# A four-layer encoder trunk on one core: other places for the modulation sums, the biases, the pooling product, and the second attention's key projection first

## The chip, the cores and the metric

The kernel runs on one core of one Trainium2 chip. The metric is device time in microseconds of one execution. Each time is the median of several runs; beside them one execution was taken by the hardware profiler, and all rows below come from that one. The engines: PE (TensorE, matmuls; PEld are its weight loads), DVE (VectorE), ACT (ScalarE), POOL (GpSimd), SP (SyncE, which issues most transfers).

## The reference

The input is x of 256 tokens by 1024 channels, one conditioning vector c, and the weights of four layers. Layer i mixes tokens by i mod 3: 0 is latent attention (layers 0 and 3), 1 a convolution module (layer 1), 2 a pooling mixer (layer 2); each is followed by a squared-ReLU feed-forward of width 4096.

```
c_act = silu(c)
for i in range(4):
    sh_m, sc_m, gt_m, sh_f, sc_f, gt_f = split(c_act @ ada_w[i] + ada_b[i], 6)
    h = rmsnorm(x, g0) * (1 + sc_m) + sh_m
    y = attention(h) | conv(h) | pool(h)
    x = x + gt_m * rmsnorm(y, g1)
    h = rmsnorm(x, g2) * (1 + sc_f) + sh_f
    x = x + gt_f * rmsnorm(relu(h @ w1) ** 2 @ w2, g3)
```

The attention projects h down to 384 columns for the queries and 256 + 32 for keys and values, norms both, projects them up for 16 heads, and applies a rotary embedding to 32 columns of each head. The convolution module is a gated product of 1024 to 2048 columns, 31 causal taps per channel, a layer norm, silu and a product of 1024 by 1024 with bias. The pooling mixer takes windowed means less the token, and multiplies four groups of 256 channels by their own matrix, with bias and scale.

## The kernel before, in words

The tokens are two tiles of 128. Every float32 product is made of three passes in the fp32r form: a weight is split into a high part (`A.copy`, L173) and a low part (`V.tensor_tensor`, L174), so is each activation, and a product is high by high, low by high and high by low (`mm3`, L582). So every weight tile of 512 KB that arrives costs ScalarE and DVE about a microsecond each. Weights go through five buffers (`NRAW`), their halves through six each (`NHL`).

**Boundaries.** `boundary` (L522) stands between any two sub-layers: squares of y, root on POOL, residual, squares of x, root, scaled tokens, transposes. The two tiles go one after the other. `line` fixes the order on an engine. For the convolution and the feed-forwards a `headblock` runs the first weight block for tile 0 ahead of tile 1's transposes; for the second attention and the pooling mixer nothing stands there. The pooling mixer hands in `tokens` and `early` in place of transposes.

**Modulation.** `c_act @ ada_w` is cut into 88 units of 1 MB that run beside the layers (8 more at the start): unit n is piece n mod 8 of a row group; the groups are, by layer, (g0, g1, g2) and then (g0, g2, g1). `ada(n)` takes n units at the places that the lists `MIX` and `FF` give: for a mixer the units at its places, those in the boundary ahead of it, and those fetched ahead; for a feed-forward the units after each of 16 chunks, and the same two. A unit is either 4 matmuls on PE, or two accumulates on DVE (L221, L223), after which one flush (`ada_flush`) multiplies the sums on PE. In feed-forwards and in the convolution the units go to DVE, in boundaries and in the pooling mixer to PE. After the last piece the row goes through DVE and, when it is needed, over DRAM into a broadcast tile (`spread`, two transfers on POOL's queue).

**Buffers of the units.** There are four (`NADA`). A unit's transfer is issued by SP, and SP issues in the order in which the program is written; it waits for a free buffer, and what stands behind it waits too. In a feed-forward `ada_fetch(ahead)` stands at chunk 14 (`CF`), behind the chunk's own unit and ahead of the fetch of the second-product weights of chunk 13. `tc.issue_after(gli.ins)` puts a chunk's units on DVE behind its `gl` (L710).

**Feed-forward** (L682): 16 chunks of 256 hidden columns; chunk c's first product (`colhalf`, L646), relu, square, halves; then the second product of chunk c - 1 (`rowblock`, L660) into four banks `y`; the last one takes chunks 14 and 15.

**Second attention** (L786): `down` runs the keys' and the queries' down projections in turn, two pieces of 128 rows at a time; then both are normed (`stats`, `normed`, `gained`).

**Convolution** (L1040): eight blocks of the gated product with the taps of an earlier block between them, then the last taps, layer norm (`un`), transposes, silu, and the product with `w_pw2` in two halves; its bias is 8 matmuls with one row, high and low.

**Pooling mixer** (L1177): means by a band matrix on PE, halves, then for each tile its bias (4 one-row float32 matmuls in the trace) and 24 matmuls of 256 columns.

## Time and profile before

| what | us |
|---|---|
| median of 3 runs | 1178.71 (1175.62 to 1179.85) |
| the profiled execution | 1184.47 |
| its span, first to last instruction | 1182.6 |
| PE busy | 1138.4 |
| PEld busy | 923.5 |
| DVE busy | 850.6 |
| ACT busy | 645.3 |

Engines run beside each other; PE's busy time counts an instruction until its modelled end, and overlapping ones once. The mean granted TensorE clock of this execution is 0.983 of full speed (2.4 GHz). The stages, by the span: first attention to 157 us, feed-forward 0 to 340, convolution to 470, feed-forward 1 to 662, pooling mixer to 690, feed-forward 2 to 883, second attention to 988, feed-forward 3 to the end.

### The profile page before, as it was taken

Reading aid. Unit: us, or ns where it says so; the run is one execution under the profiler, and the core shown is the slowest. Engines: PE = TensorE matmul, PEld = TensorE weight load, DVE = VectorE, ACT = ScalarE, POOL = GpSimd, SP = SyncE. Lnnn points to the kernel's source line nnn. Section 1 sums busy time; section 2 is a strip of 40 time slices with the busy share of each in tenths; the row PEclk is TensorE's granted clock in tenths of the full one; section 3 lists DMA queues with packets and bytes.
Section 4 is the critical chain, followed back from the end, with each engine's and each line's share of the span. In section 5 each row is a group of like instructions: output and inputs, shape, how many; then the busy total and the mean of one; then the engine's idle time right before and its main releaser. Section 6 shows DMA issues by size and latency. Waiting matters only on the chain. (4 is left out here: it accounts for less than half of the span.)

```text
span 1182.6 us, 17593 instructions
## 1 busy us (share of the span) xinstructions
PE 1138.4 (96%) x6706; PEld 923.5 (78%) x6706; DVE 850.6 (72%) x1197; ACT 645.3 (55%) x1145; POOL 54.1 (5%) x127
## 2 busy tenths in 40 slices
PE   7899999999999999999999999999997999999997
PEld 4667778788778867888887677878877878888886
DVE  3689787877766665787876778787876995755554
ACT  3355576556553244755564366555545675756553
POOL 1000010000010010000000110000011001000000
PEclk9999999999999988999999899999998999999999
DMA  9878759787617785778896479888644522766550
GB/s 332 304 290 311 298 208 347 270 329 290 245 53 236 256 322 213 272 272 351 315 343 256 187 278 364 311 311 323 246 134 157 170 81 80 250 199 191 183 193 35
DMA packets 73383, 290.00 MB, mean 245 GB/s; under 512 B 9986, under 2 KB 15234, under 8 KB 61012
## 3 DMA queue, kind: packets, MB, share of 16 engines
q1 hardware_dynamic: 70484, 280.44, 65.1%
q0 software_dynamic: 2816, 8.46, 2.0%
q8 instruction: 52, 0.85, 0.3%
q14 instruction: 31, 0.25, 0.1%
HBM read 286.57 MB, written 2.29 MB: 244 GB/s over the span
## 5 line engine op out<-in xcount | busy, mean ns | idle before, releaser
L174 DVE TENSOR_TENSOR lo<-raw,hi 128x1024 fp32r<-128x1024 f32 (+2 forms) x335 | 392.0, 1192 | 98.4 <-ACT hi L173 69.0
L173 ACT CAST hi<-raw 128x1024 fp32r<-128x1024 f32 (+2 forms) x335 | 335.1, 1028 | 78.6 <-PE y L587 39.4
L652 PE MATMUL h<-hT,hi 128*128 128x512 f32 x960 | 240.4, 392 | 0.0
L652 PEld LDWEIGHTS h<-hT,hi 128*128 128x128 f32 x960 | 175.8, 188 | 37.7 <-issue 3.4
L583 PE MATMUL y<-hi,gh 128*128 128x512 f32 x512 | 200.3, 393 | 1.5 <-ACT hi L173 1.5
L586 PE MATMUL y<-lo,gh 128*128 128x512 f32 x512 | 200.1, 391 | 0.2
L587 PE MATMUL y<-hi,gl 128*128 128x512 f32 x512 | 199.0, 390 | 0.0
L655 PEld LDWEIGHTS h<-hT,lo 128*128 128x128 f32 x960 | 131.0, 190 | 14.9 <-issue 5.9
L704 ACT COPY r<-h 128x256 f32<-128x256 f32 x120 | 44.5, 371 | 175.8 <-PE h L655 175.7
L655 PE MATMUL h<-hT,lo 128*128 128x256 f32 x960 | 136.0, 283 | 0.0
L223 DVE SCALAR_TENSOR_TENSOR acc<-araw,c_act,acc 128x1024 f32<-128x1024 f32 x106 | 130.7, 1279 | 0.4 <-DMA araw<-in_ada_w_dram 0.4
L583 PEld LDWEIGHTS y<-hi,gh 128*128 128x128 f32 x512 | 96.3, 188 | 22.8 <-ACT hi L173 2.4
L587 PEld LDWEIGHTS y<-hi,gl 128*128 128x128 f32 x512 | 96.1, 188 | 21.8 <-issue 0.8
L586 PEld LDWEIGHTS y<-lo,gh 128*128 128x128 f32 x512 | 96.4, 188 | 18.5 <-DVE lo L174 1.0
L705 DVE TENSOR_TENSOR r<-h,r 128x256 f32<-128x256 f32 x120 | 50.5, 421 | 39.8 <-ACT r L704 39.2
L710 DVE TENSOR_TENSOR gl<-r,gh 128x512 fp32r<-128x512 f32 x60 | 41.4, 690 | 50.2 <-ACT gh L709 50.2
L706 ACT ACTIVATE r<-r 128x512 f32<-128x512 f32 x60 | 37.9, 632 | 35.2 <-DVE r L705 35.2
L583 PE MATMUL y<-hi,hT 128*128 128x512 f32 x96 | 39.4, 412 | 0.0
L707 ACT ACTIVATE r<-r 128x512 f32<-128x512 f32 x60 | 37.9, 632 | 1.7
L586 PE MATMUL y<-lo,hT 128*128 128x512 f32 x96 | 38.8, 405 | 0.0
L587 PE MATMUL y<-hi,hT 128*128 128x512 f32 x96 | 38.6, 404 | 0.0
L709 ACT CAST gh<-r 128x512 fp32r<-128x512 f32 x60 | 37.2, 620 | 1.4
(257 smaller groups left out, 1486.8 us busy)
## 6 DMA issues: line engine op xcount, KB each, us to landing
raw<-in_w_dram SPq DMA_DIRECT2D x256, 512.0 KB, 5.8
araw<-in_ada_w_dram SPq DMA_DIRECT2D x96, 1024.0 KB, 6.4
raw<-in_w_pw_dram SPq DMA_DIRECT2D x24, 512.0 KB, 5.7
raw<-in_w_o_dram SPq DMA_DIRECT2D x16, 512.0 KB, 3.2
u<-ud SPq DMA_DIRECT2D x32, 132.0 KB, 2.8
raw<-in_w_ukv_dram SPq DMA_DIRECT2D x8, 512.0 KB
bc_g<-rowd POOLq DMA_DIRECT2D x8, 512.0 KB, 4.0
bc_a<-rowd POOLq DMA_DIRECT2D x7, 512.0 KB, 6.7
```

Of the source, the lines that this page charges most:

```text
L173: put(A.copy(h, raw), "act")
L174: put(V.tensor_tensor(l, raw, h.bitcast(F32), op=ALU.subtract), "dve")
L223: V.scalar_tensor_tensor(acc, raw[:, sl], ck, acc, op0=ALU.mult, op1=ALU.add)
L583: mm = T.matmul(o, ah, bh, start=start, stop=False, skip_group_check=True)
L586: T.matmul(o, ah, bl, start=False, stop=False, skip_group_check=True)
L587: return T.matmul(o, al, bh, start=False, stop=stop, skip_group_check=True)
L652: T.matmul(b, w(0, kk), pair[:, :, kk], start=(kk == 0), stop=False, skip_group_check=True)
L655: T.matmul(b[:, 0:S], w(1, kk), pair[:, 0, kk], start=False, stop=(kk == KT - 1), skip_group_check=True)
L704: A.copy(rf, hb[:, S:])
L705: V.tensor_tensor(rf, hb[:, 0:S], rf, op=ALU.add)
L706: A.activation(r, r, AF.Relu)
L710: gli = V.tensor_tensor(gl, g2, gh.bitcast(F32), op=ALU.subtract)
```

## The change

- A finished modulation row is written to DRAM at once (`stage`); a broadcast is then one transfer.
- The four matmuls of a unit or flush stand in the order 2, 3, 0, 1 and are chained.
- The pooling boundary: the second tile's y-squares come ahead of the first tile's means; the casts of the means, the first tile's bias and the high part of its product come between the second tile's steps; the mixer's order on PE is written out.
- Biases of convolution and pooling: `bias_rows` puts high and low on rows 0 and 32 of one tile; 2 matmuls per token tile with a `ones_r` of 33 rows, in the convolution in the middle of the product.
- The convolution fetches the first four pieces of `w_pw2` in its loop, and broadcasts and turns the next rows at m == 2; its ninth place for units is gone.
- The pooling constants are fetched ahead of feed-forward 1 and not in its chunk 12; the first weights of feed-forward 2 ahead of the units.
- The lists of units: fewer in boundaries and mixers, more in the feed-forwards 0 and 1, and there up to chunk 14.
- The second attention: `downblock` loads two of the four key pieces ahead of the boundary, runs them for tile 0 ahead of tile 1's transposes, then the other three quarters, then norms the keys; the queries' projection follows. One of the two key banks comes from the "h" banks.

```
@@ -244,6 +244,10 @@
...
+        for j in ((0, 1) if g == 1 else (1,)):
+            stage(i, g, j)
+        if (i, g) == (2, 0):
+            stage(i, g, 0)
@@ -261,9 +265,13 @@
...
-        for j in range(4):
+        mm = None
+        for j in (2, 3, 0, 1):
+            prev = mm
...
+            if prev is not None:
+                nosync(mm, prev)
@@ -538,15 +552,16 @@
...
-            if tokens is not None:
-                tokens(xa, r)
-                low = early()
-            else:
+            if tokens is None:
...
+        if tokens is not None:
+            tokens(xa, r)
...
+        if tokens is not None:
+            low = early()
@@ -561,13 +576,17 @@
...
+        if tokens is not None:
+            low[0][0]()
...
+            low[1][0]()
+            early()
...
-            low[0]()
+            low[0][1]()
...
-            low[1]()
+            low[1][1]()
@@ -657,6 +676,19 @@
...
+    def bias_rows(src, gain=None):
+        raw = raws.tile([P, D], F32, tag="raw", name="bias")[0:33]
+        G.memset(raw, 0.0)
+        for p in (0, 32):
+            nc.sync.dma_start(raw[p:p + 1], src)
+        if gain is not None:
+            V.tensor_tensor(raw, raw, gain[0:33], op=ALU.mult)
+        r = raws.tile([P, D], F32R, tag="raw", name="bias_r")[0:33]
+        A.copy(r, raw)
+        V.tensor_tensor(r[32:33], raw[32:33], r[32:33].bitcast(F32), op=ALU.subtract)
+        return r
@@ -783,7 +815,32 @@
...
-    def mla(i, h, units, ahead):
+    def downblock(w, hh, hl):
+        src, width = w.rearrange("p k n -> p (k n)"), KVL + ROPE
+        parts = [load(src[:, width * kk:width * (kk + 2)]) for kk in (0, 2)]
+        bs = []
+        def run(t, ks):
+            if len(bs) == t:
+                bs.append(bank("y" if t else "h", f"ck{t}"))
+            ts = slice(t * P, (t + 1) * P)
+            for low in range(2):
+                for kk in ks:
+                    if kk // 2 == len(parts):
+                        parts.append(load(src[:, width * kk:width * (kk + 2)]))
+                    wh, wl = parts[kk // 2]
+                    c = slice((kk % 2) * width, (kk % 2 + 1) * width)
+                    for st, mv in ((hl, wh),) if low else ((hh, wh), (hh, wl)):
+                        line("pe", T.matmul(bs[t][:, :width], st[:, kk, ts], mv[:, c],
+                                            start=(not low and kk == 0 and mv is wh),
+                                            stop=(low == 1 and kk == KT - 1),
+                                            skip_group_check=True))
+            return bs
+        return run
+    def mla(i, h, units, ahead, first=None):
@@ -850,11 +907,21 @@
...
-            dkv = down(w_dkv[j].rearrange("p k n -> p (k n)"), KVL + ROPE, "ck")
...
-            for _ in range(4):
-                ckb = next(dkv)
-                cqb = next(dq)
+            if first is None:
+                dkv = down(w_dkv[j].rearrange("p k n -> p (k n)"), KVL + ROPE, "ck")
+                for _ in range(4):
+                    ckb = next(dkv)
+                    cqb = next(dq)
+            else:
+                first(1, (0, 1, 2, 3))
+                first(0, (4, 5, 6, 7))
+                ckb = first(1, (4, 5, 6, 7))
+                last.clear()
+                rk = stats(ckb, KVL)
+                ckh, ckl = gained(normed(ckb, KVL, rk, "ck"), kg, "ck")
+                for _ in range(4):
+                    cqb = next(dq)
@@ -1087,6 +1157,12 @@
...
+                else:
+                    for k in range(2):
+                        fetch(w_pw2[j, 2 * (m + 2 - KT) + k])
+                if m == 2:
+                    prep(i, 2)
+                    shift_rows()
@@ -1109,39 +1185,32 @@
-            b2h, b2l = load(b_pw2[j])
             wp = [load(w_pw2[j, k]) for k in range(4)]
+            bias = bias_rows(b_pw2[j])
+            ada_flush()
...
-            prep(rows[(i, 2)])
-            shift_rows()
...
-            ada(units[8])
-            ada_flush()
...
-                for n in range(2):
-                    ns = slice(512 * n, 512 * n + 512)
-                    T.matmul(y[t][n], ones_r, b2h[:, ns], start=True, stop=False, skip_group_check=True)
-                    T.matmul(y[t][n], ones_r, b2l[:, ns], start=False, stop=False, skip_group_check=True)
@@ -1158,7 +1227,11 @@
...
-                     [sl_[:, k] for k in range(4)], y, False, False, tiles_first=True)
+                     [sl_[:, k] for k in range(4)], y, True, False, tiles_first=True)
+            for t in range(NT):
+                for n in range(2):
+                    T.matmul(y[t][n], ones_r, bias[:, 512 * n:512 * n + 512], start=False,
+                             stop=False, skip_group_check=True)
@@ -1206,73 +1276,94 @@
...
+        def product(t, low):
+            ts = slice(t * P, (t + 1) * P)
+            for g in range(4):
+                for k in range(2):
+                    ws = slice((2 * (g % 2) + k) * 256, (2 * (g % 2) + k) * 256 + 256)
+                    for q in ((0, 1), (0,))[low]:
+                        line("pe", T.matmul(y[t][g // 2][:, 256 * (g % 2):256 * (g % 2) + 256],
+                                            (ph, pl)[low][:, 2 * g + k, ts], wp[g // 2][q][:, ws],
+                                            start=False, stop=(low == 1 and k == 1),
+                                            skip_group_check=True))
+        def biased(t):
+            for n in range(2):
+                line("pe", T.matmul(y[t][n], ones_r, bias[:, 512 * n:512 * n + 512],
+                                    start=True, stop=False, skip_group_check=True))
+        y = []
+        spilt = []
-            low = [means(0, h) for h in range(2)]
-            ahead1.append(means(1, 0))
-            return low
+            if not spilt:
+                parts = [means(0, h) for h in range(2)]
+                spilt.append(spill(0))
+                return parts
+            y.extend(y_banks())
+            biased(0)
+            product(0, 0)
...
         head(tokens=tokens, early=early)
+        for k in range(2):
+            fetch(w1[i, 0, k])
+        ada_fetch(ahead)
+        spilt.append(spill(1))
+        parts = [means(1, h, spilt[h]) for h in range(2)]
+        for high, _ in parts:
+            high()
+        for _, low in parts:
             low()
         gate["free"] = 0
+        gate_row(i)
+        prep(i, 2)
+        biased(1)
+        product(0, 1)
+        product(1, 0)
+        product(1, 1)
         ada(units)
...
     MIX = {
         0: ([2, 4, 2, 3, 3, 2], 0, 1),
-        1: ([0, 0, 2, 0, 1, 2, 1, 0, 1], 2, 3),
-        2: (2, 4, 3),
+        1: ([0, 0, 2, 1, 1, 1, 1, 0, 0], 1, 3),
+        2: (1, 4, 2),
         3: ([0, 0, 0, 0, 0, 0], 0, 0),
     }
     FF = {
-        0: ([1, 1, 1, 1, 1, 2, 1, 1, 1, 1, 1, 1, 1, 1, 0, 0], 1, 3),
-        1: ([1, 1, 1, 2, 1, 1, 2, 1, 1, 2, 1, 1, 1, 1, 0, 0], 2, 4),
-        2: ([1, 1, 1, 1, 2, 1, 2, 1, 2, 1, 1, 2, 1, 2, 1, 0], 2, 0),
+        0: ([1, 2, 1, 1, 2, 1, 1, 2, 1, 1, 2, 1, 1, 2, 1, 0], 1, 3),
+        1: ([2, 1, 1, 2, 1, 1, 2, 1, 1, 1, 1, 1, 1, 1, 1, 0], 2, 4),
+        2: ([1, 1, 1, 1, 1, 1, 1, 1, 1, 1, 2, 1, 1, 2, 2, 0], 1, 0),
         3: ([0] * NFC, 0, 0),
     }
     qgs = cp.tile([P, q_g.shape[0], 3], F32, name="qgs")
@@ -1299,6 +1390,9 @@
...
+            elif s:
+                run = downblock(w_dkv[i // 3], hi, lo)
+                first = [lambda t: run(t, (0, 1, 2, 3)), run]
```

Left out are the calls that pass (i, g, j) in place of a row, `ones_r` with 33 rows, `spill` and `means` (the two halves of the former `means`), and the transfer of the pooling constants.

## Rows read from the trace of the kernel before

**Rows 1.** The page's first part: busy time, share, instructions.

```profile
PE 1138.4 (96%) x6706; PEld 923.5 (78%) x6706; DVE 850.6 (72%) x1197; ACT 645.3 (55%) x1145; POOL 54.1 (5%) x127
```

**Rows 2.** Stretches: busy PE, PEld, DVE, ACT, POOL; granted clock, DMA share, GB/s.

```profile
436.70:450.40 13.70, 13.70 (x42) 8.69 (x35) 7.54 (x14) 7.06 (x18) 1.17 (x2) 0.50 0.86 348
450.40:468.60 18.20, 18.20 (x82) 15.00 (x80) 10.69 (x12) 7.47 (x14) 1.56 (x3) 1.00 0.62 232
...
672.20:682.50 10.30, 10.30 (x36) 7.53 (x35) 4.96 (x9) 0.96 (x3) 3.22 (x6) 0.50 0.67 277
...
890.70:894.10 3.40, 3.40 (x15) 2.83 (x15) 2.14 (x7) 2.59 (x9) 1.52 (x3) 0.50 0.17 46
```

**Rows 3.** Timeline of PE, feed-forwards 0 and 1: start us, us, what, [idle before].

```profile
221.02 1.05 PE L265 MATMUL adap<-acc,ones_c 128*32 128x512 f32 x4
...
222.67 1.05 PE L265 MATMUL adap<-acc,ones_c 128*32 128x512 f32 x4
...
309.32 0.39 PE L652 MATMUL h<-hT,hi 128*128 128x512 f32 x1
...
631.37 1.98 PE L652 MATMUL h<-hT,hi 128*128 128x512 f32 x8
...
637.01 1.07 PE L265 MATMUL adap<-acc,ones_c 128*32 128x512 f32 x8
639.60 1.19 PE L583 MATMUL y<-hi,gh 128*128 128x512 f32 x4 [1.52 <-ACT hi L173]
```

**Rows 4.** Timeline of PE, the convolution's product and the units behind it.

```profile
439.44 0.78 PE L583 MATMUL y<-hi,hT 128*128 128x512 f32 x1
...
468.87 1.92 PE L265 MATMUL adap<-araw,c_act 128*32 128x512 f32 x16
```

**Rows 5.** Timeline of ACT in the pooling mixer.

```profile
668.64 0.60 ACT L135 ACTIVATE junk<-y 128x512 bf16<-128x512 f32 x1
...
685.31 0.60 ACT L135 ACTIVATE junk<-y 128x512 bf16<-128x512 f32 x1
```

**Rows 6.** Timeline of PE in the pooling mixer.

```profile
673.32 3.78 PE L1251 MATMUL y<-raw,ones_f 1*128 1x512 f32 x4
```

**Rows 7.** Timeline of DVE at the convolution's tail.

```profile
433.16 2.35 DVE L174 TENSOR_TENSOR lo<-raw,hi 128x1024 fp32r<-128x1024 f32 x2
...
436.42 0.81 DVE L1132 TENSOR_SCALAR un<-ctok,mv,r 128x512 f32<-128x512 f32 x1
```

**Rows 8.** Waits of PE, 877 to 920 us: total us, times, longest.

```profile
PE hT_ps L412 <- DVE xa L406: 3.6, 1, 3.6
PE cqT L836 <- DVE cn L832: 2.5, 1, 2.5
```

**Rows 9.** Timeline of DVE behind the second attention's boundary.

```profile
894.99 3.82 DVE L174 TENSOR_TENSOR lo<-raw,hi 128x576 fp32r<-128x576 f32 x5
```

**Rows 10.** Timeline of DVE, accumulates of chunk 13 in feed-forwards 0 and 1.

```profile
309.07 2.47 DVE L223 SCALAR_TENSOR_TENSOR acc<-araw,c_act,acc 128x1024 f32<-128x1024 f32 x2
...
629.55 2.48 DVE L223 SCALAR_TENSOR_TENSOR acc<-araw,c_act,acc 128x1024 f32<-128x1024 f32 x2
```

**Rows 11.** Timeline of SP, feed-forwards 0 and 1, issues merged.

```profile
289.09 10.18 SPq L197 DMA_DIRECT2D araw<-in_ada_w_dram  x3
299.37 2.64 SPq L155 DMA_DIRECT2D raw<-in_w_dram  x5
...
623.21 9.17 SPq L197 DMA_DIRECT2D araw<-in_ada_w_dram  x2
632.48 8.68 SPq L155 DMA_DIRECT2D raw<-in_w_dram  x6
```

**Rows 12.** The page's transfers: count, KB each, us to landing.

```profile
raw<-in_w_o_dram SPq DMA_DIRECT2D x16, 512.0 KB, 3.2
```

**Rows 13.** Timeline of ACT, chunk 14 of feed-forward 1.

```profile
637.99 0.63 ACT L706 ACTIVATE r<-r 128x512 f32<-128x512 f32 x1 [0.49 <-DVE r L705]
...
640.95 1.05 ACT L173 CAST hi<-raw 128x1024 fp32r<-128x1024 f32 x1 [0.87 <-DMA raw<-in_w_dram]
```

More of the change, by code (lines that the diff above doesn't have):

```diff
@@ L312, in tile_trunk, with stage, spread, bcast @@
     bct = {}
-    def spread(t, row, j):
-        d = dr.tile([2, 512], F32, tag="row", name="rowd")
-        ins = nc.gpsimd.dma_start(d, row[64 * j:64 * j + 64:32])
+    staged = {}
+    def stage(i, g, j):
+        d = dr.tile([2, 512], F32, tag="row", name="rowd", bufs=8)
+        nc.gpsimd.dma_start(d, rows[(i, g)][64 * j:64 * j + 64:32])
+        staged[(i, g, j)] = d
+    def spread(t, i, g, j):
+        ins = nc.gpsimd.dma_start(t, staged.pop((i, g, j)).rearrange("a n -> (a n)").unsqueeze(0)
+                                  .to_broadcast([P, D]))
         if gate["pool"] is not None:
             nosync(ins, gate["pool"])
-        nc.gpsimd.dma_start(t, d.rearrange("a n -> (a n)").unsqueeze(0).to_broadcast([P, D]))
-    def bcast(tag, row, j):
+    def bcast(tag, i, g, j):
         t = act.tile([P, D], F32, tag=f"bc_{tag}", name=f"bc_{tag}")
-        spread(t, row, j)
+        spread(t, i, g, j)
         bct[tag] = t
@@ L332, in gate_row, with prep @@
             sent.add(i)
-            bcast("g", rows[(i, 1)], 0)
-    def prep(row):
-        bcast("a", row, 1)
-        bct["sh"] = row
+            bcast("g", i, 1, 0)
+    def prep(i, g):
+        bcast("a", i, g, 1)
+        bct["sh"] = rows[(i, g)]
     def shift_rows(row=None):
@@ L684, in ffn @@
         pair = both[0]
-        bcast("g", rows[(i, 1)], 1)
+        bcast("g", i, 1, 1)
         y = None
@@ L1118, in conv @@
                     taps(*p, dg, t * P, P)
-            prep(rows[(i, 2)])
-            shift_rows()
             sh_, sl_ = planes()
@@ L1192, in pool @@
             fetch(pool_w[j, k])
-        fetch(pool_b[j])
         wp = [load(pool_w[j, k], gains) for k in range(2)]
-        bias = fetched.pop((pool_b[j].tensor.name, pool_b[j].offset))
-        V.tensor_tensor(bias, bias, psc[0:1, :], op=ALU.mult)
+        bias = bias_rows(pool_b[j], psc)
         hs = []
@@ L1242, in pool @@
+        head(tokens=tokens, early=early)
+        for k in range(2):
[6 more added lines that the diff above has]
+        for _, low in parts:
             low()
         gate["free"] = 0
-        bcast("g", rows[(i, 1)], 0)
-        prep(rows[(i, 2)])
-        ada(units)
-        y = y_banks()
-        for t in range(NT):
-            ts = slice(t * P, (t + 1) * P)
-            for n in range(2):
-                T.matmul(y[t][n], ones_f[0:1], bias[:, 512 * n:512 * n + 512], start=True,
-                         stop=False, skip_group_check=True)
-            for low in range(2):
-                for g in range(4):
-                    for k in range(2):
-                        ws = slice((2 * (g % 2) + k) * 256, (2 * (g % 2) + k) * 256 + 256)
-                        for q in ((0, 1), (0,))[low]:
-                            T.matmul(y[t][g // 2][:, 256 * (g % 2):256 * (g % 2) + 256],
-                                     (ph, pl)[low][:, 2 * g + k, ts], wp[g // 2][q][:, ws],
-                                     start=False, stop=(low == 1 and k == 1),
-                                     skip_group_check=True)
@@ L1323, in tile_trunk @@
                 args = (i, (hi, lo), sched[0], sched[2])
-                y = mla(*args) if i % 3 == 0 else conv(*args, first)
+                if i % 3 == 0:
+                    y = mla(*args, first and first[1])
+                else:
+                    y = conv(*args, first)
 def layout(inp):
```

61 lines of the change are left out of this document (32 added, 29 removed).

## The prediction

> **What bounds the kernel now.** I read the page's engine lines first. The matrix engine (PE) is busy 96% of the span [rows 1]; the vector engine (DVE) is at 72%. So time can come only from matmuls that go away, from gaps of PE, and from its clock. Next the clock by stretches [rows 2]: PE ran at 1.2 GHz (0.50) for 13.7 us at the convolution's tail, for 10.3 us in the pooling mixer, and for 3.4 us after the second attention's boundary; at 0.50 a matmul takes twice its time, so 82 matmuls in 18.2 us (0.222 us each) at full clock is what the same work costs elsewhere. Then the timelines of PE, of the sync queue (SP) and of DVE around every place that the diff touches. The feed-forwards (four, some 177 us each) run without gaps but for two things: the flushes of the modulation sums, and the end of the second one, where PE waited 1.52 us for a weight [rows 3].
>
> **What the change is worth, part by part.** All sums are against the profiled execution.
>
> *Flushes.* A flush multiplies the summed pieces of the modulation into one bank. Before, its two halves come apart: 4 matmuls of 1.05 us for each half, where the whole one at 637.01 takes 1.07 us [rows 3]; of the eight flushes in the feed-forwards seven are split. The new order (2, 3, 0, 1, chained) puts them together. By the new lists, units 17 to 36 go to feed-forward 0, 46 to 63 to 1 and 70 to 87 to 2, so there are nine flushes, one of which falls into a hold (below). 7 x 2 x 1.05 - 8 x 1.07 = 6.1 us; the ends of the halves overlap with what follows, so I take 5.5. Bounds: 0 if the halves still wait apart, 7.2 if no flush were added.
>
> *Units off PE.* Two units on PE took 1.92 us [rows 4]; four fewer run there. One stands ahead of the convolution: 0.9 us; the others are inside the sums below.
>
> *The pooling mixer.* Before, the square of the second tile's y starts on ScalarE at 668.64, behind the two casts of the first tile's means, and the first tile's product ends so late that its squares start at 685.31 [rows 5]. The new boundary puts the y-square ahead of the means (some 4.5 us earlier), then the residual, squares and root; I step this forward with the same durations and get the second tile's tokens at 672.1 rather than 675.1, the means by 674.0, the four bias matmuls and the first tile's low part (8 of about 0.12 us) by 675.5. That is 9.8 us before 685.31. The bias at half clock alone took 3.78 us in the second tile [rows 6]; it becomes two 33-row matmuls. I take off 0.6 us (the bias now needs a cast and a subtraction ahead of the chain on ScalarE and DVE) and 1.2 us for clock still lost: 8.0. What is late next is the scaled identity for the first tile's transposes, as now: the chain behind the y-squares is not shortened. Bounds: 3 (only the bias gets cheaper) to 10.2.
>
> *The convolution's tail.* The dense product starts at 439.44 [rows 4], because the second half of `un` came at 436.42, behind two weight splits (2.35 us from 433.16) on DVE [rows 7]. These weights are now fetched inside the loop and split earlier, so I expect the start at 436.0. From there: 96 matmuls x 0.222 = 21.3, 12 transposes at about 0.12 = 1.5, 4 bias matmuls 0.9, and one low stretch of 3.4 us, which costs 1.7: to 461.4, against 468.87 [rows 4]. The flush that moves there costs about 1.0: 6.5 us. Bounds: 3.4 (the clock stays low as long) to 9. The prep and shift rows that move to m == 2 cost their 8 small matmuls there as they did here: nothing won, nothing lost.
>
> *The second attention.* PE waited 3.6 us for the second tile's scaled tokens [rows 8]. Half of the first tile's key projection, 12 matmuls of 288 columns (about 0.13 us), fills 1.6 of these. But the third and fourth pieces of these weights are split only behind the chain: DVE does five such splits in 3.82 us from 894.99 [rows 9]. Before, PE had the query projection's first piece to go on with; now all key matmuls come first, so PE waits about 2 us there: the filled 1.6 is paid back. What remains is the 2.5 us wait for the query's normed values [rows 8]: the 24 key and value matmuls of 0.12 us that came behind it can now run in it, since the keys' values are normed while the query's projection runs. I take the whole wait, 2.5 us. Bounds: -2.5 (a longer wait on the splits, nothing won) to 4.
>
> *End of feed-forward 2.* Two chunks in a row with two units: each adds 4 accumulates of 1.24 us to DVE [rows 10]. I charge 1.5 us (0 to 4).
>
> *The holds.* This speaks against the change. SP issues in the order written, and the fetch of a unit waits until DVE has used the unit four before it. At c == 14 the feed-forward fetches 3 or 4 units ahead, and the weights for the chunk's products stand behind them. Before, in feed-forward 0, three such fetches issued between 289.09 and 299.27 and the weights at 299.37; in 1, SP stood from 623.21 to 632.38 and the weights went out at 632.48, just after DVE ended its accumulates at 632.0 [rows 10, 11]. PE then started at 639.60, 7.1 us after the issue [rows 3, 11]. With the new lists the unit that has to be used is, in 0, the second of chunk 13 (before: chunk 12's), and in 1 that of chunk 14 itself (before: chunk 13's).
>  - Feed-forward 0: accumulates from 309.07 [rows 10], now 4 of 1.24: 314.0; issue 314.4. PE's column matmuls of chunk 14 start at 309.32 and take 5.6 (631.37 to 637.01 [rows 3]), so PE is free at 314.9. PE resumes at 314.4 + 7.1 = 321.5. At the least it is the 3.2 us in which an output weight lands [rows 12] and a cast of 1.0 [rows 13]: 318.6. So 3.7 to 6.6; I take 5.0.
>  - Feed-forward 1: PE is free at 637.0, relu and square follow (637.99), and without the weight cast that stood between them (640.95) [rows 13] gl is there at 640.6, the accumulates end at 643.0, issue 643.4, PE resumes between 647.6 and 650.5, against 639.60: 8.0 to 10.9; I take 9.6, since five weights and a unit are again issued at once, as they were at 632.48.
>  - After each of the two holds I charge one low stretch like that at 890.70 (3.4 us, costs half): 2.4 for both, since part of it is wait anyhow.
>  Together 17.0 us lost, where the rows before lost 1.5.
>
> *Rest.* Staging the rows in DRAM when they are made takes a transfer out of later broadcasts; no PE wait of before hangs on those, so nothing. Queued behind the staged transfer on POOL are the roots; at the places of staging no root is due.
>
> Sum: 5.5 + 0.9 + 8.0 + 6.5 + 2.5 - 1.5 = 21.9 won, 17.0 lost: 4.9 us faster. The profiled execution took 1184.47 us; so 1179.6, and as the median (1178.71) lies 5.8 below it, 1174.
>
> One rule speaks against the flush term. The row shows the two halves 1.05 us each, between other matmuls [rows 3]. The Trainium skill ("TensorE: Matmul & The Clock Gate", Part 2, What happens when you issue a matmul) says that matmuls stay in program order and only weight loads are pulled ahead. So a chained flush holds everything behind it until the last accumulate is there; that is the rival "flushes wait", which is worked out from rows below.
>
> **The rivals.**
>  - *The clock stays up.* Neither the pooling mixer, the convolution nor the holds lower it: 2.2 + 2.8 + 2.4 = 7.4 us more: 1166. For it: the single-row matmuls that stood ahead of both low stretches are gone. Against: a gap of 3.6 us was followed by a low stretch [rows 2, 8], and the holds are longer.
>  - *No hold.* The accumulates come early or the queue passes: 21.9 us, so 1157. For it: in feed-forward 0 of before SP was held until 299.27 [rows 11], and PE worked on without a wait until 309.32 [rows 3]. Against: 632.0 and 632.48 [rows 10, 11].
>  - *The holds decide* (slower). Place: chunk 14 of feed-forwards 0 and 1. Price: the long ends 6.6 + 10.9, and behind them a clock that stays down as long as in the two long stretches (10.3 and 13.7 us [rows 2], half of each: 12.0): 29.5 - 21.9 = 7.6 us slower: 1186. It decides from 22 us on.
>  - *Flushes wait.* Each of nine waits one accumulate of 1.24 us more [rows 10]: 11.2 us, so 6.3 slower: 1185.
>  - *The key part does nothing.* Its 1.6 us are paid back and the query's wait stays: 2.5 less: 1176.
>
> **How the numbers follow.** A measurement tells about 0.5% (5.9 us) from no change. Chances: forecast 0.33 (its own range 1166 to 1181; a third of it faster, the rest same), clock stays up 0.20 (faster), no hold 0.13 (faster), holds decide 0.22 (mostly slower), flushes wait 0.05 (slower or same), key part 0.07 (same). Faster 0.44, same 0.32, slower 0.24. For 8 in 10 the range reaches from "no hold" to a little beyond "holds decide": 1157 to 1189.
>
> **What would show it.** In feed-forward 1's chunk 14: SP's weight issues about 0.4 us after the last accumulate and a PE wait of 8 to 11 us on the cast; in 0 one of 4 to 6. Flushes of 8 matmuls in 1.07 us with nothing between. In the pooling mixer the first tile's y-squares 8 us nearer to the mixer's start. In the convolution the first dense matmul some 3 us nearer to the last tap. In the second attention the 3.6 us wait at about 2, a new wait of about 2 on the splits, and no 2.5 us wait before the query's transposes. The prediction is wrong if SP's weight issues at chunk 14 don't follow the accumulates, or if the mixer's product is still bound by the second tile's chain.

## The result, and the profile after

The changed kernel takes 1187.62 us (median of 5 runs, 1185.27 to 1189.70), the kernel before 1178.71 on the same chip. The ratio is 1.0079 with a 95% interval from 1.0057 to 1.0101, so it is slower by some 9 us where 5 us faster was forecast; it lies inside the range that was given. The profiled execution took 1185.27 us.

PE is a little less busy than in [rows 1], in a span that is longer: what was added is waits. The page's first part of the changed kernel:

```profile
span 1183.5 us, 17602 instructions
PE 1120.2 (95%) x6682; PEld 916.8 (77%) x6682; DVE 858.7 (73%) x1206; ACT 647.3 (55%) x1146; POOL 56.9 (5%) x129
```

The timeline of PE in the changed kernel at chunk 14 of feed-forwards 0 and 1 (columns as in [rows 3]) shows the two holds:

```profile
310.54 1.11 PE L674 MATMUL h<-hT,lo 128*128 128x256 f32 x8
316.58 1.55 PE L602 MATMUL y<-hi,gh 128*128 128x512 f32 x3 [4.92 <-ACT hi L173]
...
632.86 1.11 PE L674 MATMUL h<-hT,lo 128*128 128x256 f32 x8
639.98 1.94 PE L271 MATMUL adap<-acc,ones_c 128*32 128x512 f32 x8 [6.01 <-DVE acc L223]
648.37 1.22 PE L602 MATMUL y<-hi,gh 128*128 128x512 f32 x2 [6.45 <-ACT hi L173]
```

What SP and DVE did there (SP's timeline, then DVE's and ACT's, of the same kernel; they answer to [rows 10, 11, 13]):

```profile
306.63 2.72 SPq L197 DMA_DIRECT2D araw<-in_ada_w_dram  x2
309.44 10.79 SPq L155 DMA_DIRECT2D raw<-in_w_dram  x7
...
628.95 11.34 SPq L197 DMA_DIRECT2D araw<-in_ada_w_dram  x2
640.38 9.55 SPq L155 DMA_DIRECT2D raw<-in_w_dram  x6
```

```profile
304.12 4.87 DVE L223 SCALAR_TENSOR_TENSOR acc<-araw,c_act,acc 128x1024 f32<-128x1024 f32 x4
...
637.46 2.47 DVE L223 SCALAR_TENSOR_TENSOR acc<-araw,c_act,acc 128x1024 f32<-128x1024 f32 x2
```

```profile
647.27 1.04 ACT L173 CAST hi<-raw 128x1024 fp32r<-128x1024 f32 x1 [10.46 <-DMA raw<-in_w_dram]
```

The accumulates end at 308.99 and 639.93; SP issues the weights 0.45 us later both times, and PE goes on 7.1 and 8.0 us behind that issue. In [rows 3, 11] it was 7.1.

The four stretches of low clock between 300 and 710 us of the changed kernel (columns as in [rows 2]; the granted clock is the number ahead of the DMA share, 0.50 is 1.2 GHz):

```profile
316.70:323.50 6.80, 6.12 (x14) 4.38 (x15) 6.58 (x6) 4.86 (x5) 0.00 (x0) 0.50 0.93 336
443.00:446.40 3.40, 3.40 (x11) 2.72 (x10) 3.24 (x7) 3.40 (x10) 0.00 (x0) 0.50 0.02 7
637.60:654.70 17.10, 8.23 (x22) 4.72 (x23) 9.93 (x10) 6.28 (x6) 1.06 (x2) 0.50 0.78 280
695.60:702.40 6.80, 6.12 (x25) 5.46 (x26) 3.64 (x7) 2.81 (x8) 0.74 (x2) 0.50 0.04 16
```

Two of them are new and begin inside or right behind the holds: 6.8 and 17.1 us. The one at the convolution's tail is 3.4 us long instead of 13.7. The one of 10.3 us inside the pooling mixer is gone, and 6.8 us stand behind the mixer, at the boundary into feed-forward 2.

To put the runs side by side I cut each trace where the second tile's transposes begin at a boundary (into feed-forward 0, the convolution, feed-forward 1, feed-forward 2, the second attention, feed-forward 3). The table is worked out from the traces of PE: the stage's time without half of the time in which PE worked at 0.50, and that half behind the plus sign. The pooling mixer lies in the stage of feed-forward 1.

```
                       FF0          conv         FF1+pool     FF2     2nd attention
before                 191.3        121.6 + 6.8  215.7 + 5.1  192.3   104.7 + 4.9
before, 2nd profile    191.3        122.3        215.3 + 3.4  192.2   104.4 + 4.1
after                  194.8 + 3.1  123.2 + 1.7  221.1 + 7.2  188.4   104.7 + 3.3
flush alone            188.8        121.5        213.4 + 3.4  188.4   104.9 + 3.3
lists alone            197.1 + 2.7  125.0 + 8.5  231.3 + 8.9  192.9   105.0 + 3.4
units earlier          189.4        123.0 + 3.4  211.3 + 3.3  187.9   104.4 + 3.4
units + early gate     189.4        123.6 + 3.1  209.9 + 1.7  187.8   104.7 + 3.4
old lists and conv     189.1        122.1        214.3 + 4.1  190.2   104.7 + 4.9
```

Without the clock a stage repeats within some 0.7 us from execution to execution (the first two rows); with it, the same code differs by 6.1 (the convolution, 128.4 and 122.3). All ratios below are against the kernel before, measured beside the run; 0.1% is 1.2 us. They are taken from the fast executions; two of the twelve of the run with the flush alone, at 1843 and 3863 us, were slow ones.

### The profile page after: what moved, and what is told of

Read it like the earlier page. It is cut to its first block, busy times and chain, and to the rows that moved or that the text cites. A ratio compares the mean times of both kernels' runs of the same rounds, so it can differ in the third digit from the quotient of the medians.

```text
span 1183.5 us, 17602 instructions
## 1 busy us (share of the span) xinstructions
PE 1120.2 (95%) x6682; PEld 916.8 (77%) x6682; DVE 858.7 (73%) x1206; ACT 647.3 (55%) x1146; POOL 56.9 (5%) x129
## 4 chain that ended last, share of the span: by engine, by line
PE 76%; DVE 9%; ACT 5%; DMA 4%; issue 3%; POOL 2%; SPq 0%; POOLq 0%; DVEq 0%; ACTq 0%
PE h L671 16%; PE y L602 10%; PE y L605 10%; PE y L606 10%; PE h L674 8%; DMA raw<-in_w_dram 3%; PE adap L271 2%; PE dw_ps L1130 2%; DVE acc L223 2%; ACT junk L135 2%; DVE lo L174 2%; PE s_ps L1042 2%; PE h L645 1%; PE pw L619 1%; PE pw L621 1%
## 5 line engine op out<-in xcount | busy, mean ns | idle before, releaser
L174 DVE TENSOR_TENSOR lo<-raw,hi 128x1024 fp32r<-128x1024 f32 (+1 forms) x334 | 391.5, 1193 | 101.4 <-ACT hi L173 65.7
L173 ACT CAST hi<-raw 128x1024 fp32r<-128x1024 f32 (+1 forms) x334 | 335.1, 1028 | 109.2 <-PE y L606 46.1
L223 DVE SCALAR_TENSOR_TENSOR acc<-araw,c_act,acc 128x1024 f32<-128x1024 f32 x110 | 135.7, 1279 | 0.0
L606 PEld LDWEIGHTS y<-hi,gl 128*128 128x128 f32 x512 | 97.5, 190 | 21.1 <-DVE gl L742 0.2
L602 PE MATMUL y<-hi,hT 128*128 128x512 f32 x96 | 39.0, 406 | 0.0
L528 DVE TENSOR_TENSOR v<-y,bc_g 128x512 f32<-128x512 f32 x32 | 21.9, 688 | 22.0 <-ACT junk L135 20.5
```

Source lines behind the costliest of these rows:

```text
L173: put(A.copy(h, raw), "act")
L174: put(V.tensor_tensor(l, raw, h.bitcast(F32), op=ALU.subtract), "dve")
L223: V.scalar_tensor_tensor(acc, raw[:, sl], ck, acc, op0=ALU.mult, op1=ALU.add)
L602: mm = T.matmul(o, ah, bh, start=start, stop=False, skip_group_check=True)
L606: return T.matmul(o, al, bh, start=False, stop=stop, skip_group_check=True)
```

## The experiments

**Are the holds the loss?** First the fetch ahead moved by a chunk:

```diff
-CF = 14
+CF = 15
```

> The changed kernel, in which the feed-forward fetches its 3 or 4 units ahead one chunk later (at c == 15, behind the weights of chunk 15 instead of ahead of the output weights of chunk 13). Theory 'the holds': the two waits of PE for an output weight's cast (4.92 us in feed-forward 0; 6.01 and 6.45 us in feed-forward 1) go, and with them the low clock behind them (6.8 and 17.1 us at 0.50 in the changed kernel, half of each 12.0): 17.4 + 12.0 = 29.4 us less than 1187.6, so 1158. Rival 'the wait alone': the clock falls there anyway: 1187.6 - 17.4 = 1170. Rival 'the hold moves': the last four output weights now stand behind the units and come as late: within 4 us of 1187.6.

Measured: 1173.5 us, ratio 0.9951 (0.9923 to 0.9980). The waits at chunk 14 are gone (1.4 us is left in feed-forward 1, as before the change), but SP then stood from 616.67 to 637.58 in front of the last output weights and the pooling mixer's, and PE waited 3.95 us for the mixer's tokens. Part of the hold moved, as the third theory said, but only a part. The second way leaves the fetch and moves the unit:

```diff
-        0: ([1, 2, 1, 1, 2, 1, 1, 2, 1, 1, 2, 1, 1, 2, 1, 0], 1, 3),
-        1: ([2, 1, 1, 2, 1, 1, 2, 1, 1, 1, 1, 1, 1, 1, 1, 0], 2, 4),
+        0: ([1, 2, 1, 1, 2, 1, 1, 2, 1, 2, 2, 1, 2, 1, 0, 0], 1, 3),
+        1: ([2, 1, 1, 2, 1, 1, 2, 1, 1, 2, 1, 1, 1, 1, 0, 0], 2, 4),
```

> The changed kernel with the unit of chunk 14 moved forward in both lists (feed-forward 0: chunks 9 to 15 take 2, 2, 1, 2, 1, 0, 0; feed-forward 1: chunk 9 takes 2 and chunk 14 none), so that the unit whose buffer the last fetch ahead needs was used a chunk earlier; the place of the fetch stays. Theory 'the holds': as with the later fetch, about 1158; if some 1.5 us of wait stay in feed-forward 1, as in the kernel before, 1160. Rival 'the wait alone': 1170. Rival 'too many units for DVE' (the accumulates themselves delay the splits, wherever they stand): within 4 us of 1187.6.

Measured: 1166.72 us, ratio 0.9894 (0.9868 to 0.9919). Against the changed kernel that is 1.0079 / 0.9894, so 21.8 us for three units taken one to five chunks earlier. SP's and PE's timeline in feed-forward 1 of this run, then two stretches around the places of the holds:

```profile
606.55 20.46 SPq L197 DMA_DIRECT2D araw<-in_ada_w_dram  x3
627.11 12.77 SPq L155 DMA_DIRECT2D raw<-in_w_dram  x8
```

```profile
626.76 1.06 PE L271 MATMUL adap<-acc,ones_c 128*32 128x512 f32 x8
...
634.33 1.20 PE L602 MATMUL y<-hi,gh 128*128 128x512 f32 x4 [1.41 <-ACT hi L173]
```

```profile
300.00:330.00 30.00, 30.00 (x159) 24.93 (x158) 23.29 (x26) 15.79 (x24) 0.00 (x0) 1.00 0.77 279
625.00:650.00 25.00, 23.53 (x121) 18.61 (x120) 17.76 (x22) 14.30 (x20) 2.02 (x3) 1.00 0.74 274
```

SP still stands for 20 us, but it gets free while PE has the flush (whole, 1.06 us) and the chunk's column matmuls to do; of the 7.2 us from the issue to the product only 1.41 are waited for, and the clock stays at 1.00. The time lies between the two theories (1158 and 1170): the waits and the clock behind them both went, and the rest of the change is worth less than the forecast had it.

The other side is the kernel before with the new lists and nothing else:

```diff
-        1: ([0, 0, 2, 0, 1, 2, 1, 0, 1], 2, 3),
-        2: (2, 4, 3),
+        1: ([0, 0, 2, 1, 1, 1, 1, 0, 0], 1, 3),
+        2: (1, 4, 2),
...   (and the three new lists of FF)
```

> The kernel before with nothing but the new lists of units (MIX and FF). Theory 'the holds': 17.4 - 1.5 us of wait and 12.0 of low clock on top of 1178.7, less 0.9 for a unit off PE: 1206, with a wait of about 5 us in feed-forward 0 and about 12 in feed-forward 1. Rival 'the lists are harmless and the rest of the change (staged rows, the new order of the boundary) made the loss': 1177 to 1181.

Measured: 1207.23 us, ratio 1.0241 (1.0203 to 1.0279), as the first theory had it. The same two waits stand in it, PE's waits over the whole run (total us, times, longest):

```profile
PE adap L265 <- DVE acc L223: 11.1, 3, 4.8
PE hT_ps L395 <- ACT dg L389: 8.9, 2, 8.5
...
PE y L583 <- ACT hi L173: 6.7, 1, 6.7
```

The 8.5 us in front of feed-forward 2 were not expected: DVE waited 4.93 us there for the broadcast of the gate row, whose copy in DRAM is made only in the mixer. So the lists do all of the loss, and with these lists the rest of the change wins (1187.6 against 1207.2); how much it wins without them, the other runs say.

**The key part.** The changed kernel with `first = None` for the second attention:

> The changed kernel without the keys' part: the second attention again projects keys and queries in turn behind the boundary. Theory 'the key part fills the wait for the second tile's tokens': PE waits 3.6 us again instead of 1.9, and the time is 1.5 to 2 us above the changed kernel: 1189.4. Rival 'its 1.7 us are paid back by the wait for the query (2.68 us)': no difference, 1187.6. Rival 'it costs': 1185.

Measured: 1188.05 us, ratio 1.0075 (1.0051 to 1.0100): no difference, the first rival. PE's waits from 880 to 925 us, first in the changed kernel, then without the key part:

```profile
PE cqT L893 <- DVE cn L889: 2.7, 1, 2.7
PE hT_ps L426 <- DVE xa L420: 1.9, 1, 1.9
PE ckT L893 <- DVE cn L889: 0.7, 1, 0.7
PE cq L602 <- ACT hi L173: 0.6, 1, 0.6
```

```profile
PE hT_ps L426 <- DVE xa L420: 3.8, 2, 3.6
PE cqT L893 <- DVE cn L889: 2.5, 1, 2.5
...
PE ckT L893 <- DVE cn L889: 0.2, 1, 0.2
```

The half tile of keys takes 1.7 us off the first wait, and 0.6 + 0.5 + 0.2 come back behind it. The 2.7 us wait for the query stayed, because the 24 key and value matmuls stand behind the query's transposes in PE's order. This run puts them ahead:

```diff
+                v0 = keys(0)
-            cq = normed(cqb, QL, rq, "cq", gate["ada"] if units[0] else None)
+            cq = normed(cqb, QL, rq, "cq", gate["ada"] if units[0] else gate["kv"] if v0 else None)
...   (gate["kv"] is the last value matmul; the keys' rope moves ahead of it)
```

> The changed kernel with the units taken earlier (1166.7) and, in the second attention, the first group's keys and values (24 matmuls) put ahead of the query's transposes in PE's order; their data are there 5 us before those transposes can run. Theory 'PE's order keeps the 2.7 us wait for the query': the wait goes below 0.5 us and the time falls by 2 to 2.7 us: 1164.3. Rival 'paid back' (the banks and copies of the keys come to stand in the query's chain): 1166.7. In the first attention the order is as it was.

Measured: 1168.59 us, ratio 0.9907 (0.9881 to 0.9934) beside 0.9894 for the units earlier: nothing won. PE's waits from 860 to 920 us of this run:

```profile
PE pT_ps L1070 <- DVE p L1059: 2.1, 1, 2.1
PE cqT L893 <- DVE kT L913: 1.4, 1, 1.4
PE ckT L893 <- DVE cn L889: 0.9, 1, 0.9
PE k_ps L606 <- DVE lo L174: 0.6, 1, 0.6
```

The query's wait now ends with the copy of the keys, which DVE does ahead of the normed query, and the first transposes of p wait 2.1 us instead of 1.1. Paid back, as the rival said.

**The flush.** The kernel before with the new order of its four matmuls:

```diff
-        for j in range(4):
+        mm = None
+        for j in (2, 3, 0, 1):
+            prev = mm
...
+            if prev is not None:
+                nosync(mm, prev)
```

> The kernel before with nothing but the new order of a flush's four matmuls (2, 3, 0, 1, each behind the last). Forecast: of eight flushes in the feed-forwards seven are split into two of 1.05 us, so 5.5 us less than 1178.7: 1173. Rival 'the halves still wait apart': 1178.7. Rival 'flushes wait': the chained flush holds PE for the last accumulate, 1.24 us in each: about 1182 to 1184.

Measured: 1174.38 us, ratio 0.9948 (0.9923 to 0.9972), 6.1 us less; the forecast was 5.5. The flush that stood at 221.02 and 222.67 in [rows 3] is one row in this run's timeline of PE, and another one shows the price of the chain, a wait of 0.59 us for the last accumulate:

```profile
219.33 1.06 PE L267 MATMUL adap<-acc,ones_c 128*32 128x512 f32 x8
...
307.42 1.07 PE L267 MATMUL adap<-acc,ones_c 128*32 128x512 f32 x8 [0.59 <-DVE acc L223]
308.41 0.50 PE L656 MATMUL h<-hT,hi 128*128 128x512 f32 x1
```

**The gate row.** In the run with the units earlier DVE waits 1.81 us for the broadcast gate row at the boundary into feed-forward 2, and PE 3.94 us for what hangs on it. The early issue:

```diff
                 spilt.append(spill(0))
+                gate_row(i)
                 return parts
```

> The changed kernel with the units taken earlier (1166.7) and the broadcast of the pooling mixer's gate row issued right behind the last use of its buffer, some 4 us sooner than now. Theory 'the gate row is late': in the trace with the units taken earlier VectorE waits 1.81 us for that row at the boundary into feed-forward 2 (scaled y at 675.20), ScalarE 3.99 us behind it and PE 3.94 us; with the row there, PE's wait falls to about 2.1 us, and the low clock behind it (6.8 us) gets shorter or goes: 1166.7 - 1.8 - (0 to 3.4) = 1161.5 to 1165. Rival 'the roots are late anyway': the root of y is there at 674.3, 0.9 us before the row's use, so only 0.9 us or less is won: 1166.

Measured: 1162.22 us, ratio 0.9862 (0.9837 to 0.9886), and once more, later:

> The run with the units taken earlier and the early gate row once more, on the same chip as the three others: 1162 as before (ratio 0.986), if the gain of 4.5 us on the units taken earlier was not one chip's; 1165 (1.8 less than 1166.7) if only the wait itself was won.

Measured: 1162.45 us, ratio 0.9864 (0.9844 to 0.9884). This is the fastest kernel of the study, 1.4% under the kernel before. First DVE's row and PE's in the changed kernel, then in the second of these runs:

```profile
690.79 1.29 DVE L528 TENSOR_TENSOR v<-y,bc_g 128x512 f32<-128x512 f32 x2 [1.32 <-DMA bc_g<-rowd]
...
696.28 2.08 PE L409 MATMUL hT_ps<-dg,xa 128*128 128x128 f32 x8 [3.82 <-ACT dg L403]
```

```profile
667.82 1.28 DVE L528 TENSOR_TENSOR v<-y,bc_g 128x512 f32<-128x512 f32 x2
...
672.92 1.16 PE L409 MATMUL hT_ps<-dg,xa 128*128 128x128 f32 x8 [2.04 <-ACT dg L403]
```

The wait and a part of the low clock behind it (6.8 us, now 3.4) went, 3.0 us in the stage table (1.4 and 1.6). The ratio fell by 3.8 us (0.9894 to 0.9862), and its interval still overlaps that of the units earlier; 3.0 of the 3.8 are what the traces show, the rest may be the start (below).

**The convolution.** First its bias alone in the old form, on top of the units earlier:

> The changed kernel with the units taken earlier (1166.7) and, in the convolution, the bias of the dense product again as two matmuls of one row for each bank, ahead of the product (8 in all in place of 4 of 33 rows behind the first half). Theory 'the one-row matmuls lower the clock': the low stretch at the convolution's tail is 10 to 14 us long again, as in the kernel before (13.7), instead of 3.4: 5 us slower, and 4 more matmuls of 0.22 us: 1172. Rival 'the clock fell there for another reason': the stretch stays at 3.4 us, and as the eight matmuls fall into the 2.5 us wait for the transposes, the time stays at 1166.7.

Measured: 1168.45 us, ratio 0.9909 (0.9885 to 0.9933), no difference that can be told; the low stretch there was 6.8 us long in the profile, between the two theories. Then the whole mixer as before, on top of the early gate:

> The changed kernel with the units taken earlier and the early gate row (1162.2), and the whole convolution mixer as in the kernel before (bias rows of one partition ahead of the product, weights fetched and split behind the last taps, shift rows and flush at the end, one unit on PE there). Theory 'the new convolution costs': without the low clock it takes about 1.5 us more than the old one (stage from the first tile transpose to the next: 128.4 - 6.9 = 121.5 before, 126.7 - 3.4 = 123.3 with the early gate row; 121.5 with the flush alone, where the clock did not fall): 1160.7. Rival 'the forecast's term': the new one wins 6.5 us: 1168.7.

Measured: 1172.12 us, ratio 0.9938 (0.9918 to 0.9958): slower by 9 us, beyond the rival's 6.5. But its trace doesn't put that into the convolution: the stage takes 123.2 us without the clock there, 123.6 with the new code. Then the same with a unit more on PE in front of feed-forward 2:

> As the run with the old convolution, and one unit of feed-forward 2 taken from its first chunk's accumulates to PE, at the boundary in front of it (2 there in place of 1). Theory: the unit's 16 matmuls... 8 matmuls of about 0.12 us each run in the 2.0 us wait for the scaled identity, so nothing is lost on PE, and the clock does not fall behind a wait of 1 us (1.2 us in the kernel before): 1.7 us less than the run with the old convolution, 1159. Rival 'the unit comes late or the wait was not the clock's cause': no difference, 1160.7.

Measured: 1167.24 us, ratio 0.9897 (0.9879 to 0.9915), 4.9 us less than the run before it. PE's wait in front of feed-forward 2 did fall, from 2.04 to 1.18 us, but the stage up to it is no shorter in the profiles (211.1 against 210.7 without the clock), so where the 4.9 us come from isn't shown. Meanwhile a second profile of the kernel before:

> The kernel before once more, for a second profile. Theory 'the long low stretches belong to the execution, not to the code': the 13.7 us at the convolution's tail are shorter by 3.4 us or more, or absent, and the other stages keep their times once half of the low clock is taken off. Rival 'they belong to the code': 13.7 us within 3.4 us again, and about 10 us in the pooling mixer.

Measured: 1174.39 us. The convolution's tail from its last taps on, in two stretches, against [rows 2], and the pooling mixer's stretch (the place that answers to 436.70 there is at some 435.2 here, inside the first stretch):

```profile
427.90:441.60 13.70, 12.37 (x160) 8.09 (x151) 10.32 (x17) 6.64 (x18) 3.07 (x6) 1.00 1.00 404
441.60:459.80 18.20, 18.20 (x83) 15.04 (x82) 11.56 (x14) 10.11 (x18) 1.30 (x2) 1.00 0.89 333
664.40:674.70 10.30, 10.30 (x51) 8.23 (x53) 6.28 (x11) 2.56 (x7) 3.21 (x6) 0.67 0.66 273
```

With the same code, one-row bias matmuls and all, the clock at the convolution's tail never fell, and the convolution took 122.3 us where it had taken 121.6 + 6.8. Over all profiles the old code of this mixer shows 13.7 us of low clock behind its last taps twice, 6.8 and 3.4 once each and none three times; the new code shows 3.4 us eight times and 6.8 once. In the pooling mixer the first theory held only in part: 6.8 us of low clock came again where it had been 10.3, and 6.8 in the run with the flush alone too.

**The whole change but the lists, with and without the convolution's part.** MIX and FF as in the kernel before:

> The changed kernel with the units' lists of the kernel before, so the whole change but the lists (the convolution's last unit stands one chunk earlier, on VectorE). Theory 'the lists made the whole loss': as with the units taken earlier, 1164 to 1168, and PE's wait in front of feed-forward 2 is about 1 us, since there are again two units there. Rival 'the lists also won something (fewer units on PE, 0.96 us each for four)': 1170.

Measured: 1174.34 us, ratio 0.9962 (0.9944 to 0.9981). Slower than both theories, and 8 us slower than with the new lists and earlier units. In its profile the convolution takes 3.8 us longer than there (126.8 without the clock), feed-forward 1 with the pooling mixer 2.1 and feed-forward 2 1.7; PE waits twice for 2.6 us in front of the convolution's taps there, by the profile for transfers. In the profile of the last run of this section, with the same lists, it waits 3.1 us for the flush of the unit that moved into the last chunk instead. That the units more on PE do the rest is likely, but no run here shows it. Beside the kernel before, the change without its lists is worth 4.5 us, no more than the flush alone (6.1). With the convolution's code of before as well:

> As the run with the old lists, and the convolution mixer as in the kernel before: what is left of the change is the flush, the staged rows, the boundary and the pooling mixer, and the key part. Theory 'the convolution's part wins nothing that an execution's clock does not bring anyway': as the old lists within 2 us, 1166. Rival 'it wins what the last comparison of medians says (1172.1 against 1162.2)': 8 to 10 us slower, 1175. Beside the run with the flush alone (1174.4, 5.2 per mille under before) this one tells what the pooling mixer is worth: forecast 8.0, so 1166; by the two traces (216.9 - 3.4 in the stage from feed-forward 1 to 2 with the flush alone, 214.6 - 3.4 with the units taken earlier) 2.3, so 1172.

Measured: 1172.10 us, ratio 0.9937 (0.9914 to 0.9960), no slower than with the new convolution, and within the uncertainty of the flush alone (0.9948). With the old lists, then, the pooling mixer's new order wins next to nothing: DVE waited 4.67 us for the gate row, because its copy in DRAM was itself late, and PE 5.08.

```profile
674.24 1.29 DVE L528 TENSOR_TENSOR v<-y,bc_g 128x512 f32<-128x512 f32 x2 [4.67 <-DMA bc_g<-rowd]
...
679.35 2.08 PE L409 MATMUL hT_ps<-dg,xa 128*128 128x128 f32 x8 [5.08 <-ACT dg L403]
```

> As the run with the old lists, with the pooling mixer's gate row broadcast early. Theory 'the gate row is late with these lists too': 1 to 2 us under the old lists, 1164. Rival 'the two units in front of feed-forward 2 hide the late row': no difference, 1166.

Measured: 1173.43 us, ratio 0.9948 (0.9925 to 0.9971), not to be told from the old lists; PE still waited 4.1 us there. With these lists DVE finishes the row only at 668.91 us, its broadcast goes out at 672.81 and DVE waits for it until 676.72, so an early issue can't help.

## Why the prediction was wrong, step by step

The sign went wrong on the sum, not on the mechanism that spoke against the change. The steps, forecast against measured:

- **Flushes**, 5.5 won: 6.1 by the run with the flush alone, 8.2 to 8.7 in its three feed-forward stages. Right. The rival "flushes wait" priced 1.24 us for each; 0.59 was seen. The Trainium skill ("TensorE: Matmul & The Clock Gate", Part 2, What happens when you issue a matmul) says that matmuls keep program order; the trace agrees at 307.42 in the run with the flush alone, where the flush waited 0.59 us for its sum and the last of eight matmuls of the column product (h<-hT,hi), the others of which stand ahead of it, started only behind it at 308.41.
- **Units off PE**, 0.9 won: no run singles it out; the stage of feed-forward 0, where it lies, takes 189.4 us with the units earlier and 188.8 with the flush alone.
- **The holds**, 14.6 of waits: 5.4 in feed-forward 0 (194.8 against 189.4; forecast 5.0) and 9.8 in 1 (221.1 against 211.3; forecast 9.6). Right, and each sign that was named is there: the issue 0.45 us behind the accumulate, 4.9 us of wait in 0, and in 1 12.5 us in two pieces (a little beyond 8 to 11, as the weight took 8.0 us from its issue to PE). The short ends of the two bounds rested on the 3.2 us of [rows 12], which is the attention's output weight; the weights of the feed-forwards stand in the same view of the kernel before with 5.8:

```profile
raw<-in_w_dram SPq DMA_DIRECT2D x256, 512.0 KB, 5.8
```

- **The clock behind them**, 2.4: 3.1 + 3.9 = 7.0 (7.2 - 3.3 in the stage of feed-forward 1). "One low stretch like that at 890.70" after each hold was 3.4 us; they were 6.8 and 17.1. This term was too small by 4.6.
- **The convolution's tail**, 6.5 won: nothing shown. The stage takes 122.7 to 123.9 us without the clock with the new code (where the lists are the new ones), 121.6 and 122.3 before. "I expect the start at 436.0", 3.4 earlier, failed: from the stage's beginning the dense product starts after 91.5 us (443.11 - 351.65) where it was 90.5 and, in the second profile, 88.6; behind the last tap after 5.4 us where it was 6.3 and 5.5. PE waits 2.6 us there for the second tile's `un`. The rest of the term was that 13.7 us of low clock become 3.4, and the second profile of the kernel before has none of them. PE in the changed kernel, then in the second profile of the kernel before:

```profile
441.95 1.50 PE L1218 MATMUL sT_ps<-ident,un 128*128 128x128 f32 x8 [2.63 <-DVE un L1207]
443.11 0.78 PE L602 MATMUL y<-hi,hT 128*128 128x512 f32 x1
```

```profile
436.93 0.47 PE L583 MATMUL y<-hi,hT 128*128 128x512 f32 x1
```

- **The pooling mixer**, 8.0 won: 2.1 (211.3 against 213.4 with the flush alone), 3.5 with the gate row early, and nothing to tell with the old lists. The mechanism held inside the mixer. The first tile's y-squares came 14.3 us behind the end of feed-forward 1's product (687.93 - 673.64) in place of 22.8 (685.31 - 662.50), 8.5 us nearer; against the second profile of the kernel before (20.7) and the flush alone (21.1) it is some 6 us, as the run with the units earlier has 15.0. What failed is what comes behind: from those squares to the second tile's transposes the boundary took 12.9 to 13.0 us in both profiles of before and with the flush alone, and 16.9 in the changed kernel, where PE waited 3.82 us in front of feed-forward 2 in place of 1.2 and worked at 0.50 behind that wait. "Staging the rows ... no PE wait of before hangs on those, so nothing" failed, since the row that had come in time behind a late mixer was late behind an early one; with the row issued early the boundary took 13.8 and 14.0. PE and ACT in the changed kernel, then PE in the kernel before (ACT's row is in [rows 5]):

```profile
673.64 3.64 PE L271 MATMUL adap<-araw,c_act 128*32 128x512 f32 x32
687.93 0.59 ACT L135 ACTIVATE junk<-y 128x512 bf16<-128x512 f32 x1
```

```profile
662.50 3.64 PE L265 MATMUL adap<-araw,c_act 128*32 128x512 f32 x32
```

- **The second attention**, 2.5 won: nothing (1188.05 without it). The key half filled its wait; the splits cost 0.6 and not 2; the query's wait stayed.
- **End of feed-forward 2**, 1.5 lost: 0.6 of wait, within what the stage can tell.
- **From the profile to the median.** The sum was worked out on an execution of 1184.47 us, and the 5.8 us by which it lay above the median were taken off its result. The second profile, 10.1 us shorter, has 9.4 less in the stages of the table, 9.3 of it clock: what made the first one long was in good part the low clock that the terms had already entered as won.

So without the holds the change is worth 12.5 us by the run with the units earlier (forecast 21.9), and the holds cost 21.8 (forecast 17.0): 9.3 slower instead of 4.9 faster. Of the 14.2 between, 9.4 are the terms won and 4.8 the holds. Three steps failed most. The convolution's term (6.5, nothing shown) entered a low stretch of one profiled execution as time that the edit takes away, and an earlier start that didn't come. The pooling mixer's (8.0, 2.1 measured) was right on the mixer and put at nothing the wait for the gate row behind it. The clock behind the holds (2.4, 7.0 measured) was taken from a stretch of 3.4 us. The rival "the holds decide" named the place, the price of the waits (17.5; 17.4 measured as waits of PE) and the time (1186), but came to it with 12.0 of clock and 21.9 won, both too large, so that its time was luck in part. In the rival "the clock stays up" the 2.2 and 2.8 are worked out nowhere; the terms themselves charge 1.2 and 1.7 for low clock. The feed-forwards' stretches are 175 to 187 us, not 177 each; nothing hangs on that.

What stays open: why the old convolution is 9 us slower with the new lists, when its stage is not. Its profiled execution, the fastest of its six, has a span 4.0 us longer than that of the early gate row (1164.6 against 1160.6), and these 4.0 lie ahead of everything that differs (the start, below); the rest is not in that execution. The clock alone is not it: at the same mean clock of 0.986 two of its executions took 1169.41 and 1171.40 us, two of the early gate row's 1159.57 and 1161.34.

## What to carry to other kernels

Before a low-clock stretch is entered as a gain, take a second profile of the same kernel: what one execution shows and the next doesn't is not the edit's to win (here 13.7 us at the convolution's tail in one and none in the next; the pooling mixer's came again at 6.8 of 10.3). When a fetch ahead is moved or its buffers get busier, look for what is queued behind it on the same queue: three units that stood one to five chunks later cost 22 us. And a chain that is made earlier makes every side input late that had been in time only because the chain was slow; list those and issue them early.

## What the runs showed of the hardware that I had not expected

The granted clock differs between executions of one kernel. At the convolution's tail of the kernel before it was at 0.50 for 13.7 us in one and at 1.00 throughout in another; over the whole span its mean was between 0.977 and 0.991 in the runs of that kernel. Around the two waits of the hold in feed-forward 1 (6.01 and 6.45 us) it stood at 0.50 for 17.1 us, from inside the first wait until 6.3 us behind the second, and for 17.1 us again without the key part and with the lists alone; behind the single wait of 4.92 us in feed-forward 0 it was 6.8 us.

The first 55 us, whose work is the same, differ between kernels: the keys' first transposes in the first attention came at 54.1 and 53.4 us in the two profiles of the kernel before, at 51.1 and 50.5 in the two of the fastest kernel, and at 50.4 to 55.5 in all. That is as large as several terms of this sum, two kernels with two profiles each suggest that it goes with the kernel more than with the execution, and no run here says why.
